# A two-layer decoder trunk on one core: fill steps laid otherwise, y gated and stored in the next head, values' weights split earlier, late weights loaded into another tile

## The chip, the cores and the metric

The kernel runs on one core of a Trainium2 chip. The time is device time in microseconds, the median of several runs; a profiled execution has a time and a trace of its own.

## The reference, cut to what matters

Two pre-norm residual layers on x of 1024 positions by 1024 channels, then a final RMSNorm. Layer 0 is a recurrent layer (RG-LRU); the change does not touch it. Layer 1 is forgetting attention with 16 heads of 64:

```python
u = h @ w_in                          # h = rms_norm(x): queries, keys, values, gate, forget logits
cum = jnp.cumsum(log_sigmoid(f_logit + b_f), axis=1)
logits = q @ k.T / 8 + (cum_q - cum_k), causal mask
p = softmax(logits)                   # per head, 1024 x 1024
o = p @ v
y = o * silu(gate)
x = x + y @ w_out
```

All is float32. The kernel takes every large product in three passes on TensorE: each operand is split into a high part (a cast, `to_hi`) and a low part (a subtraction, `to_lo`).

## The kernel before, in words

**Heads and runs.** Layer 1 loops over 16 heads (line 1116). Queries fall into two chunks of 512, c=0 and c=1, a chunk into four score rows of 128 queries. Head hd has two runs. The first weighs chunk 0 of the head (`weigh(hd, 0)`) beside the score rows 7, 6, 5, 4 of its chunk 1 (`maxima(hd, 1)`); the second weighs chunk 1 beside the score rows 3, 2, 1, 0 of the next head's chunk 0.

**The order on TensorE is written out by hand.** `ordered` walks a string: `1` is the next step of `maxima` (one score row), `0` the next step of `weigh`, `.` the next step of a generator of other work, `fill`; every matmul of a step is queued behind the last one before (`tc.issue_after(pe[0].ins)`). A fill step is six matmuls of 128x512. In heads 0 to 11 the fill is the next pair's keys, queries and gate (`kq_units`, `g_units`), 12 steps a head; later it is the output projection's partial products (`partial`). After a dot the generator `side` also takes a step.

**`maxima`, a score row:** four or two matmuls into a PSUM tile S; VectorE masks and takes the maximum in one instruction (L773); ScalarE takes the exponential with the row's sum (L778). Rows 6, 7 and 2, 3 are also turned: a block transpose on VectorE (L733), a store to DRAM, and four loads back (`pp<-turnd`, L745). The PSUM tag S has two buffers, which score rows and transposes share in turn.

**`weigh`:** its steps come in two kinds. Near rows are transposed by TensorE into a PSUM tile (`pt`), split by a cast `ph` and a subtraction `pl` (both listed as lines 87 and 98, the helpers `to_hi` and `to_lo`), and multiplied by the values in the step after. Far rows come from the DMA, are split in one step and multiplied in the next; their casts are queued behind the last exponential (`seen`), their subtractions behind the last maximum (`masked`). At the end the output is copied and added into `yo` (L903, L904).

**Gating.** `fetch_sums` loads the reciprocal sums, broadcast to 64 partitions; `scale` multiplies the gate by them and `gated` the output by the gate, both on GpSimd (L813, L913). `put_away` casts and subtracts an odd head's y and stores both parts in DRAM. Before, `settle` (beside the second run) fetches at its third step and scales and gates chunk 0 at its fourth; chunk 1 is gated after the run; the stores come in the next head's first run, at the dots 3 and 5.

**Values.** Before heads 4, 8 and 12, `values` computes the values of the next four heads. `value_weights` loads their weights in four quarters and splits each a step later.

**Weights' buffers.** All weights are loaded into the tag `wf` of three buffers and split into `wh` and `wl`, four buffers in `wpool`, two in `vwpool`. In head 14's second run `late` loads and splits, in four steps, the part of the output weights that the last pair needs.

**Queues.** Every DMA is issued by SP, in one queue, in order. The framework lists each engine's instructions ahead of time by a simulated time; it may place a load earlier than the code's order when its buffer is free.

Of the kernel before, what the change touches and what calls it, by code (L numbers as in the profile page):

```python
# [11 lines left out]
F32 = mybir.dt.float32  # L12
# [5 lines left out]
P = 128  # L18
SEQ = 1024
HALF = 512  # L20
# [3 lines left out]
HD = 64  # L24
EPS = 1e-6
GROUP = 2
ORDER = "1.0.1.10.1..0", "10.1.0.10.1.0.0"
LAST = "1..0.1..10..1..0", "10..1.0..10..1.0..0"
NEG = -1e30
PSUM = bass.MemoryType.PSUM  # L30
# [3 lines left out]
def f32(ap):  # L34
    return ap.bitcast(F32)
# [3 lines left out]
def trunk(ctx: ExitStack, tc: tile.TileContext, xt, w0, wg, wo0, pc, gn, gf, w1, wv, wf, bf, wo1, out):  # L39
    nc = tc.nc  # L40

    def pool(name, bufs, **kw):
        return tc.tile_pool(name=name, bufs=bufs, **kw)
# [7 lines left out]
    wpool = ctx.enter_context(pool("w", 4))  # L51
# [32 lines left out]
    def to_hi(hi, src, eng, scale=None):  # L84
        if eng is nc.scalar:
            if scale is None:
                nc.scalar.copy(hi, src)  # L87
            else:
                nc.scalar.activation(hi, src, AF.Copy, scale=scale)
        elif eng is nc.gpsimd:  # L90
            nc.gpsimd.tensor_scalar(hi, src, 1.0 if scale is None else scale, 0.0, ALU.mult, ALU.add)
        elif scale is None:
            eng.tensor_copy(hi, src)
        else:
            eng.tensor_scalar(hi, src, scale, None, ALU.mult)

    def to_lo(lo, src, hi, eng):
        return eng.tensor_tensor(lo, src, f32(hi), ALU.subtract)  # L98
# [80 lines left out]
    with ExitStack() as l0:  # L179
# [35 lines left out]
        k = 0  # L215
# [11 lines left out]
        def split_x(h, layer=0):  # L227
            for k, (hi, lo) in enumerate((raw, hT)[layer][h]):
                g_ = gnt[:, layer, k : k + 1]
                x = xs[h][k]  # L230
                to_hi(hi, x, nc.scalar, scale=g_)
                nc.vector.scalar_tensor_tensor(lo, x, g_, f32(hi), ALU.mult, ALU.subtract)  # L232
                yield
# [217 lines left out]
        vwpool = late.enter_context(pool("vw", 2, side="right"))  # L451
# [17 lines left out]
        for h, cs in enumerate(halves):  # L469
            y = [tuple(z[:, cs] for z in p) for p in ys[-2:]]  # L470
            hT[h] = [pair() for k in range(KT)]
            parts = split_x(h, 1)
# [29 lines left out]
    with ExitStack() as l1:  # L502
        tu = l1.enter_context(pool("tu", 1))
        at = l1.enter_context(pool("at", 2))
# [22 lines left out]
        def value_weights(g, parts):  # L527

            waiting = []
            for k in range(0, KT + 2, 2):  # L530
                if k < KT:
                    wt = wpool.tile([P, 2, 256], F32, tag="wf", name="wf", bufs=3)
                    nc.sync.dma_start(wt, wv[g, :, k : k + 2])
                    waiting.append(wt)
                if k:
                    own = wpool if k <= 4 else vwpool
                    hi = own.tile([P, 2, 256], F32R, tag="wh", name="wh")
                    lo = own.tile([P, 2, 256], F32R, tag="wl", name="wl")
                    with tc.issue_after(seen[0].ins):
                        to_hi(hi, waiting[0], nc.scalar)  # L540
                    with tc.issue_after(masked[0].ins):
                        to_lo(lo, waiting.pop(0), hi, nc.vector)
                    parts += [(hi[:, i], lo[:, i]) for i in range(2)]
                yield

        def values(g, parts):

# [260 lines left out]
        def scale(hd, cs=slice(0, SEQ)):  # L808
            rows = slice((hd % 2) * HD, (hd % 2 + 1) * HD)
            for b in range(cs.start, cs.stop, HALF):  # L810
                part = slice(b, b + HALF)
                sg = sgs[hd // 2][rows, part]
                nc.gpsimd.tensor_tensor(sg, sg, recs[hd // 2][rows, part], ALU.mult)  # L813
# [93 lines left out]
        def gated(hd, c, sub=slice(0, HALF)):  # L907

            if hd % 2 == 0:
                return  # L910
            pair = hd // 2
            yo = yos[pair, c][:, sub]
            nc.gpsimd.tensor_tensor(  # L913
                yo, yo, sgs[pair][:, c * HALF + sub.start : c * HALF + sub.stop], ALU.mult
            )
            if hd == 15:
                split_y(c, pair, yo, sub)

        def put_away(hd, c):
            if hd % 2 == 0 or hd > 12:  # L920
                return
            pair = hd // 2
            yo = yos[pair, c]
            yh = at.tile([P, HALF], F32R, tag="xp", name="yh", bufs=2)
            with tc.issue_after(seen[0].ins):
                to_hi(yh, yo, nc.scalar)
            with tc.issue_after(masked[0].ins):
                to_lo(yo.bitcast(F32R), yo, yh, nc.vector)
            for part, y in enumerate((f32(yh), yo)):
                nc.sync.dma_start(y1d[c, pair, part], y)  # L930

        def settle(hd):
            yield
            yield
            with tc.issue_after(written[0].ins):
                fetch_sums(hd)
            yield
            scale(hd)
            gated(hd, 0)

        def put_later(hd):
            for c in range(2):
                yield
                yield
                put_away(hd, c)

        def beside(*gens):
            for _ in itertools.zip_longest(*gens):
                yield
# [5 lines left out]
        def chain(*gens):  # L955
            for g in gens:
                yield from g
# [21 lines left out]
        def split_y(c, pair, y, sub=slice(0, HALF)):  # L979
            yh, yl = (z[:, sub] for z in (pair_of_y(c, pair) if sub.start == 0 else y1[c][pair]))  # L980
            to_hi(yh, y, nc.scalar)
            to_lo(yl, y, yh, nc.vector)
# [102 lines left out]
        def late():  # L1085

            for half in range(2):
                wh, wl = (kqpool.tile([P, 8, P], F32R, tag=f"qk{p}{half}", name=f"wo{p}") for p in "hl")
                for b in range(2):
                    wt = wpool.tile([P, 4, P], F32, tag="wf", name="wf", bufs=3)  # L1090
                    for d in range(2):
                        nc.sync.dma_start(wt[:, 2 * d : 2 * d + 2], wo1[half * 4 + b * 2 + d, :, 6:8])
                    sl = slice(4 * b, 4 * b + 4)

                    with tc.issue_after(seen[0].ins):
                        to_hi(wh[:, sl], wt, nc.scalar)
                    to_lo(wl[:, sl], wt, wh[:, sl], nc.vector)
                    yield
                late_w.append((wh, wl))
# [16 lines left out]
        for hd in range(HEADS):  # L1116
            pair = hd // 2
            if hd % 2 == 0:
                if hd < 12:
                    fill = kq_units(pair + 1, ((1, (0, 1)), (0, (0,))))  # L1120
                elif hd == 12:
                    pairs = ((0, 1), (2, 3), (4, 5), (6, 7))
                    todo = [(db, c) for two in pairs for c in range(2) for db in two]
                    fill = chain(
                        kq_units(7),
                        g_units(7, (0,)),
                        load_y(0),
                        first_out(),
                        g_units(7, (1,)),
                        load_y(1),  # L1130
                        partial(todo),
                        turned(0, 0),
                        turned(0, 1),
                    )
            elif pair < 6:
                fill = chain(kq_units(pair + 1, ((0, (1,)),)), late_q(hd + 1), g_units(pair + 1))
            first, second = LAST if hd > 11 else ORDER
            side = put_later(hd - 1) if hd else iter(())
            run(first, weigh(hd, 0), maxima(hd, 1), fill=fill, side=side)
            drain(side)  # L1140
            if hd == HEADS - 1:
                break
            if hd == 14:
                with tc.issue_after(seen[0].ins):
                    split_y(1, 6, yos[6, 1])
                scale(hd)
            side = late() if hd == 14 else settle(hd)
            if hd % 4 == 3 and hd < 12:

                parts = []  # L1150
                side = beside(side, value_weights(hd // 4 + 1, parts))
            run(second, weigh(hd, 1), maxima(hd + 1, 0), fill=fill, side=side)
            drain(side)
            gated(hd, 1)
            if hd == 13:
                with tc.issue_after(seen[0].ins):
                    split_y(0, 6, yos[6, 0])
            if hd < 12:
                drain(fill)
            if hd % 4 == 3 and hd < 12:  # L1160
                drain(values(hd // 4 + 1, parts))
            if hd + 2 < HEADS:
                load(hd + 2, us=(0,) if hd % 2 == 0 and hd < 12 else (0, 1))
# [84 lines left out]
```

## Time and profile before

| | |
|---|---|
| median of 3 runs | 1116.9 us (1115.07 to 1117.86) |
| the profiled execution: its time, its span | 1114.79 us, 1113.0 us |
| TensorE granted clock, mean | 0.995 |
| TensorE, VectorE, ScalarE, GpSimd busy | 98%, 71%, 52%, 15% of the span |
| DMA traffic | 145.81 MB, mean 131 GB/s |

The span runs from the first instruction to the last. A matmul's end is modelled and reaches into the next one's start, so that a busy TensorE may still lose a few tenths of a microsecond here and there; stalls are best read from start to start. In the lists of waits a line names who waited, on which line of the code, for whom, then the total, the number of times and the longest, in us. In the timeline a line has the start, the duration, the engine, the code's line, the instruction, what it writes and reads, its shape, how many were merged, and in brackets the idle time before it and what ended it. Two rows are merged where they follow each other on their engine.

### The profile page before, as it was taken

Reading aid. Unit: us, or ns where it says so; the run is one execution under the profiler, and the core shown is the slowest. Engines: PE = TensorE matmul, PEld = TensorE weight load, DVE = VectorE, ACT = ScalarE, POOL = GpSimd, SP = SyncE. Lnnn points to the kernel's source line nnn. Section 1 sums busy time; section 2 is a strip of 40 time slices with the busy share of each in tenths; the row PEclk is TensorE's granted clock in tenths of the full one; section 3 lists DMA queues with packets and bytes.
Section 4 is the critical chain, followed back from the end, with each engine's and each line's share of the span. In section 5 each row is a group of like instructions: output and inputs, shape, how many; then the busy total and the mean of one; then the engine's idle time right before and its main releaser. Section 6 shows DMA issues by size and latency. Waiting matters only on the chain.

```text
span 1113.0 us, 15892 instructions
## 1 busy us (share of the span) xinstructions
PE 1088.5 (98%) x5645; PEld 921.1 (83%) x5645; DVE 792.1 (71%) x1280; ACT 579.9 (52%) x1037; POOL 171.8 (15%) x120
## 2 busy tenths in 40 slices
PE   9999999999999999999999999999999999998997
PEld 7787888888888888987888888788888898887886
DVE  8888755876569787757887478874788757666445
ACT  8487345355454665545555355553556535434335
POOL 2312212111121201420121101111012110110010
PEclk9999999999999999999999999999999999999999
DMA  6111111111112113445767357674477845785344
GB/s 220 62 53 42 52 53 48 48 54 45 43 48 71 48 65 116 130 124 162 199 192 195 118 161 193 200 198 123 150 189 213 198 126 166 248 266 174 109 147 189
DMA packets 100919, 145.81 MB, mean 131 GB/s; under 512 B 25348, under 2 KB 53636, under 8 KB 100840
## 3 DMA queue, kind: packets, MB, share of 16 engines
q1 hardware_dynamic: 100840, 144.80, 43.6%
q8 instruction: 44, 0.72, 0.3%
q14 instruction: 35, 0.29, 0.1%
HBM read 83.48 MB, written 36.11 MB: 107 GB/s over the span
## 4 chain that ended last, share of the span: by engine, by line
PE 76%; DVE 7%; DMA 6%; issue 5%; ACT 4%; SPq 1%; POOL 1%; ACTq 0%; DVEq 0%; POOLq 0%
PE gps L57 26%; PE ops L57 16%; PE ups L57 10%; PE vps L57 7%; PE S L57 5%; PE O L57 4%; PE gate L57 3%; PE turn L57 2%; PE pt L61 2%; DVE pl L98 2%; ACT pp L778 1%; DMA T<-qkl 1%; DVE S L773 1%; DMA U<-qkh 1%; DMA turnd<-turn 1%
## 5 line engine op out<-in xcount | busy, mean ns | idle before, releaser
L57 PE MATMUL gps<-hh,wh 128*128 128x512 f32 x576 | 229.4, 398 | 0.0
L57 PE MATMUL gps<-hh,wl 128*128 128x512 f32 x576 | 225.6, 392 | 0.2 <-POOL wl L98 0.2
L57 PE MATMUL gps<-hl,wh 128*128 128x512 f32 x576 | 225.1, 391 | 0.0
L87 ACT CAST wh<-wf 128x512 fp32r<-128x512 f32 (+2 forms) x156 | 94.2, 607 | 138.0 <-PE ops L57 43.1
L98 POOL TENSOR_TENSOR wl<-wf,wh 128x512 fp32r<-128x512 f32 (+1 forms) x60 | 99.5, 1664 | 378.1 <-ACT wh L87 260.3
L57 PEld LDWEIGHTS gps<-hl,wh 128*128 128x128 f32 x576 | 108.2, 188 | 23.6
L57 PEld LDWEIGHTS gps<-hh,wl 128*128 128x128 f32 x576 | 108.7, 189 | 18.7 <-POOL wl L98 0.6
L57 PEld LDWEIGHTS gps<-hh,wh 128*128 128x128 f32 x576 | 108.5, 188 | 18.5
L813 POOL TENSOR_TENSOR sg<-sg,recb 64x512 f32<-64x512 f32 x32 | 44.4, 1407 | 487.6 <-DMA recb<-recd 445.7
L773 DVE CUSTOM_DVE_ANT_0 S<-S,mask 128x512 f32<-128x512 f32 (+7 forms) x128 | 97.0, 758 | 24.7 <-PE S L57 24.4
L778 ACT ACTIVATE pp<-S,m 128x512 f32<-128x512 f32 (+1 forms) x64 | 54.4, 851 | 87.9 <-DVE m L773 87.8
L57 PE MATMUL S<-T,U 128*128 128x512 f32 (+7 forms) x384 | 92.6, 350 | 4.0 <-ACT pp L778 4.0
L98 DVE TENSOR_TENSOR wl<-wf,wh 128x512 fp32r<-128x512 f32 x96 | 68.6, 720 | 22.6 <-ACT wh L87 22.5
L57 PEld LDWEIGHTS S<-T,U 128*128 128x128 f32 (+1 forms) x384 | 67.5, 190 | 20.8 <-ACT pp L778 9.1
L375 DVE TENSOR_TENSOR x<-x,ops 128x512 f32<-128x512 f32 x80 | 54.1, 680 | 41.2 <-PE ops L57 41.2
L57 PE MATMUL O<-pl,v 128*128 128x256 f32 (+3 forms) x302 | 77.2, 290 | 2.2 <-DMA T<-qkl 1.2
L57 PE MATMUL O<-ph,v 128*128 128x256 f32 (+3 forms) x302 | 78.8, 289 | 0.0
L57 PE MATMUL ups<-hh,wl 128*128 128x512 f32 x192 | 75.3, 392 | 0.8 <-POOL wl L98 0.8
L57 PE MATMUL ups<-hh,wh 128*128 128x512 f32 x192 | 75.7, 395 | 0.0
L57 PE MATMUL ups<-hl,wh 128*128 128x512 f32 x192 | 75.2, 392 | 0.2 <-DVE hl L232 0.2
L57 PE MATMUL vps<-wh,hh 128*128 128x256 f32 (+1 forms) x256 | 73.3, 287 | 2.0 <-DVE v L575 1.0
L57 PE MATMUL ops<-yh,wh 128*128 128x512 f32 x192 | 75.2, 392 | 0.0
(170 smaller groups left out, 2372.3 us busy)
## 6 DMA issues: line engine op xcount, KB each, us to landing
wf<-in_w SPq DMA_DIRECT2D x100, 256.0 KB
turnd<-turn SPq DMA_DIRECT2D x26, 448.0 KB
pp<-turnd SPq DMA_DIRECT2D x52, 224.0 KB
wf<-in_wo SPq DMA_DIRECT2D x64, 128.0 KB
U<-qkh SPq DMA_DIRECT2D x64, 128.0 KB
T<-qkh SPq DMA_DIRECT2D x28, 256.0 KB
turnd<-turn SPq DMA_DIRECT2D x13, 384.0 KB
pp<-turnd SPq DMA_DIRECT2D x52, 96.0 KB
```

The source lines that it names most:

```text
L57: pe[0] = nc.tensor.matmul(*args, **kw)
L61: pe[0] = nc.tensor.transpose(*args)
L87: nc.scalar.copy(hi, src)
L98: return eng.tensor_tensor(lo, src, f32(hi), ALU.subtract)
L375: nc.vector.tensor_tensor(x, x, pt, ALU.add)
L773: masked[0] = nc.vector.tensor_tensor_reduce(S[:, :n], S[:, :n], mask[:, SEQ - n :], -1.0, -NEG, ALU.add, ALU.min, accum_out=m)
L778: seen[0] = nc.scalar.activation(p, S[:, :n], AF.Exp, bias=m, scale=-1.0, accum_out=sums[:, i : i + 1])
L813: nc.gpsimd.tensor_tensor(sg, sg, recs[hd // 2][rows, part], ALU.mult)
```

## The change

- `ORDER`, the strings of heads 0 to 11, has the same steps with dots at other places: in the first run one dot moves from between the fourth score row and the last step of `weigh` to between the first step of `weigh` and the second score row; in the second run one moves from before the fourth step of `weigh` to between its first step and the second score row.
- For heads up to 11, `scale` and `gated` move from the end of the head to the first dot of the next one; the stores of y go to its fourth dot and the end of its first run.
- `value_weights` takes seven steps instead of five, the first five of them beside the head's first run. The first two quarters are split into `vwpool` and the last two into `wpool`, the other way round than before.
- In `late`, the first and third load go into the tile `turn`, which before held the score rows on their way to DRAM and is not used after head 12's second run.

```diff
-ORDER = "1.0.1.10.1..0", "10.1.0.10.1.0.0"
+ORDER = "1.0..1.10.1.0", "10..1.0.10.10.0"
...
                 if k:
-                    own = wpool if k <= 4 else vwpool
+                    own = vwpool if k <= 4 else wpool
...
                 yield
+                if k < 4:
+                    yield
...
-        def put_away(hd, c):
-            if hd % 2 == 0 or hd > 12:
+        def store_y(hd, c):
+            if hd % 2 == 0:
                 return
...
             with tc.issue_after(written[0].ins):
                 fetch_sums(hd)
-            yield
+            if hd > 11:
+                yield
+                scale(hd)
+                gated(hd, 0)
+
+        def put_away(hd):
             scale(hd)
-            gated(hd, 0)
-
-        def put_later(hd):
             for c in range(2):
-                yield
-                yield
-                put_away(hd, c)
+                gated(hd, c)
+            for c in range(2):
+                yield
+                yield
+                yield
+                store_y(hd, c)
...
                 for b in range(2):
-                    wt = wpool.tile([P, 4, P], F32, tag="wf", name="wf", bufs=3)
+                    if b:
+                        wt = wpool.tile([P, 4, P], F32, tag="wf", name="wf", bufs=3)
+                    else:
+                        wt = at.tile([P, 7 * P], F32, tag="turn", name="wf", bufs=1)[:, :HALF]
+                        wt = wt.rearrange("p (d j) -> p d j", j=P)
...
-            side = put_later(hd - 1) if hd else iter(())
+            side = put_away(hd - 1) if 0 < hd < 13 else iter(())
+            if hd % 4 == 3 and hd < 12:
+                parts = []
+                coming = value_weights(hd // 4 + 1, parts)
+                side = beside(side, itertools.islice(coming, 5))
             run(first, weigh(hd, 0), maxima(hd, 1), fill=fill, side=side)
...
             if hd % 4 == 3 and hd < 12:
-
-                parts = []
-                side = beside(side, value_weights(hd // 4 + 1, parts))
+                side = beside(side, coming)
             run(second, weigh(hd, 1), maxima(hd + 1, 0), fill=fill, side=side)
             drain(side)
-            gated(hd, 1)
+            if hd > 11:
+                gated(hd, 1)
```

## The prediction

> **What bounds the kernel now.** I read the page first, then the waits of all engines and of TensorE alone, then the timeline around each long TensorE wait.
>
> ```profile
> PE 1088.5 (98%) x5645; PEld 921.1 (83%) x5645; DVE 792.1 (71%) x1280; ACT 579.9 (52%) x1037; POOL 171.8 (15%) x120
> ```
>
> TensorE is busy 98% of the span of 1113.0 us, and the change adds and removes no matmul. All that can be won are the times in which TensorE waits. They are few:
>
> ```profile
> POOL sg L813 <- DMA recb<-recd: 445.7, 16, 45.5
> ACT wh L87 <- DMA wf<-in_w: 14.4, 7, 4.3
> PE S L57 <- ACT pp L778: 4.0, 8, 1.1
> PE ops L57 <- ACT wh L87: 3.2, 1, 3.2
> PE vps L57 <- DVE wl L98: 2.2, 3, 0.9
> PE vps L57 <- ACT wh L87: 0.6, 1, 0.6
> PE O L57 <- DMA T<-qkl: 1.2, 2, 0.7
> PE O L57 <- DVE pl L98: 0.7, 1, 0.7
> ```
>
> The columns are total us, times, longest. The reader is to see six small groups, and that none belongs to the first layer, which the change leaves alone. I count a stall from start to start, less the usual distance of two matmuls: that gives some 0.2 us more per wait than these rows, since a matmul's modelled end runs into the wait.
>
> I name the steps of a head so: S7 to S0 are the score rows (7 to 4 in the first run, 3 to 0 in the second), T a transpose step, P a product step of `weigh`, a dot one fill step. A fill step is six matmuls (a row of the chain of waits; 1.39 from start to start):
>
> ```profile
> 579.09 1.40 PE gps L57 x6
> ```
>
> **The change, part by part.**
>
> **A. Late weights.** Two of the four loads of `late()` leave the `wf` ring of three buffers for the `turn` tile, which nothing uses after head 12's second run. The timeline there:
>
> ```profile
> 1021.21 1.27 DVE L98 TENSOR_TENSOR wol<-wf,woh 128x512 fp32r<-128x512 f32 x2
> ...
> 1022.87 1.05 SPq L1092 DMA_DIRECT2D wf<-in_wo  x2
> 1024.01 1.29 SPq L108 DMA_DIRECT2D wf<-in_wo  x2
> ...
> 1025.18 0.39 PE L57 MATMUL ops<-yhl,wh 128*128 128x512 f32 x1
> 1028.72 0.79 PE L57 MATMUL ops<-yhh,wh 128*128 128x512 f32 x1 [3.15 <-ACT wh L87]
> 1029.98 0.79 PE L57 MATMUL ops<-yhh,wl 128*128 128x512 f32 x1 [0.47 <-DVE wl L98]
> ...
> 1027.47 0.62 ACT L87 CAST woh<-wf 128x512 fp32r<-128x512 f32 x1 [2.26 <-DMA wf<-in_wo]
> 1028.05 0.93 ACT L87 CAST wh<-wf 128x512 fp32r<-128x512 f32 x2
> ```
>
> The output weights of block 5 (L108) are loaded only at 1024.01, because the fourth late load (L1092, 1022.87) and they queue for ring buffers that the casts at 1021.21 give back. ScalarE then waits 2.26 us for that late load with block 5's cast behind it. TensorE loses 3.54 - 0.23 = 3.3 us, then 1.26 - 0.23 = 1.0 us. Then it runs slowly:
>
> ```profile
> 1028.70:1034.60 5.90, 5.41 (x16) 4.36 (x17) 2.05 (x5) 0.95 (x4) 0.08 (x1) 0.50 0.50 172
> ```
>
> The granted clock (third number from the end) is 0.50; of the 5.9 us 1.3 is the wait just counted, and the other 4.6 us would have taken 2.3 at full clock: 2.3 us lost. Together 6.6 us.
>
> After the change the ring serves late 2, late 4 and block 5: two of these find a buffer as soon as block 4's weights are split, long before 1021, so that the fourth late load no longer stands in front. What is late next is late 3: `turn` has one buffer, so its load waits for the first late subtraction (1021.87, the first of the pair at 1021.21), comes some 3 us later, and ScalarE may wait for it with block 5's cast behind. Bounds: 6.6 gone, or only the 1.1 us by which block 5's load moves up to 1022.9 (with a like share of the rest, 1.5). Loads here are placed ahead of the code's order when their buffer is free, so I take a value near the first: **-5.5 us**. The two loads cost no more issue time on SP than before.
>
> **B. The values' weights.** Before heads 4, 8 and 12, four quarters are loaded, cast and subtracted beside the second run, the last at its fifth dot. At the end of that run:
>
> ```profile
> 618.43 0.62 ACT L87 CAST wh<-wf 128x512 fp32r<-128x512 f32 x1 [3.39 <-DMA wf<-in_w]
> ...
> 619.31 0.61 ACT L87 CAST wh<-wf 128x512 fp32r<-128x512 f32 x1
> ...
> 620.49 0.38 PE L57 MATMUL O<-ph,v 128*128 128x256 f32 x1
> 621.79 0.39 PE L57 MATMUL vps<-wl,hh 128*128 128x256 f32 x1 [0.91 <-DVE wl L98]
> ```
>
> The last quarter's cast (619.31) stands behind a cast that waits 3.39 us for the next head's weights; the loss is 1.30 - 0.12 = 1.2 us. The wait row above has it three times with 2.2 us; with the same 0.3 added to each, and the one wait of `vps` for `wh`, 3.9 us in all. Now two quarters are split in the first run and two at the second run's first two dots, so the values' weights are there some five dots (7 us) ahead. I let a quarter of the 3.9 stand, for the cast that waits for the next head's weights is still there and holds back S0's exponential: **-2.9 us**. The price: two casts (0.62 each on ACT) and two subtractions (0.64 each on DVE, half of the pair at 1021.21) per such head into the first run, beside S6 to S4; and on SP three of the four loads come ahead of the gate's weights, whose second half then takes its ring buffer only after the first quarter is split. I hold that hidden: it is needed only at the seventh dot, after the whole first run. Bounds: -3.9, and +3.9 if it is not hidden (a rival below). Buffers: the first two quarters take the pool whose last use lies a group of heads back, the last two the free half of the other; no new wait.
>
> **C. Fill steps laid otherwise.** The first run moves a dot from before the last P to between T and S6; the second one from before P2 to between T and S2. What the even heads have there now (the first row is an odd head's, for comparison):
>
> ```profile
> 683.64 1.02 DVE L98 TENSOR_TENSOR pl<-pp,ph 128x512 fp32r<-128x512 f32 x2
> ...
> 704.79 0.40 PE L57 MATMUL gps<-hl,wh 128*128 128x512 f32 x1
> 706.26 1.09 PE L57 MATMUL S<-T,U 128*128 128x512 f32 x4 [1.07 <-ACT pp L778]
> ...
> 718.15 0.27 PE L791 MATMUL tr<-ident,sums 128*8 128x128 f32 x1
> 718.82 0.62 PE L57 MATMUL S<-T,U 128*128 128x384 f32 x2 [0.39 <-ACT pp L778]
> ...
> 715.77 0.58 ACT L903 COPY yo<-O 64x512 f32<-64x512 f32 x1 [0.39 <-DMA y1d<-yo]
> 717.97 0.70 ACT L778 ACTIVATE pp<-S,m 128x512 f32<-128x512 f32 x1
> ...
> 728.36 2.12 DVE L98 TENSOR_TENSOR pl<-pp,ph 128x512 fp32r<-128x512 f32 x2 [1.33 <-ACT ph L87]
> 728.80 2.83 POOL L813 TENSOR_TENSOR sg<-sg,recb 64x512 f32<-64x512 f32 x2 [23.57 <-DMA recb<-recd]
> ```
>
> S6 and S2 wait for the exponential of the row that holds their PSUM buffer (1.24 and 0.6 us). Of such waits the list has 8 with 4.0 us, with 0.2 added to each 5.6. A dot more (1.39) covers every one: **-5.6 us**. At the end of the head the pair of subtractions takes 2.12 us beside GpSimd's two, against 1.02 without (683.64), and the last P waits: the two last rows of the list, three heads, 2.5 us with the addition. P2 and with it these subtractions now come up to a dot earlier against GpSimd, which starts when the sums' DMA lands; I take **-1.6 us** of the 2.5.
>
> What is late next: the products that lose their dot. An odd head, which has none of these waits (the last two rows are an even head's):
>
> ```profile
> 679.51 0.86 PE L57 MATMUL S<-T,U 128*128 128x512 f32 x4
> 685.42 0.28 PE L57 MATMUL O<-ph,v 128*128 128x256 f32 x1
> ...
> 693.89 0.40 PE L57 MATMUL S<-T,U 128*128 128x256 f32 x2
> 697.60 0.28 PE L57 MATMUL O<-ph,v 128*128 128x256 f32 x1
> ...
> 695.95 0.69 DVE L98 TENSOR_TENSOR pl<-pp,ph 128x512 fp32r<-128x512 f32 x1 [1.14 <-ACT ph L87]
> ...
> 708.57 0.86 PE L57 MATMUL S<-T,U 128*128 128x512 f32 x4
> 713.30 1.02 DVE L98 TENSOR_TENSOR pl<-pp,ph 128x512 fp32r<-128x512 f32 x2
> ```
>
> First run: from S5 (679.51) to the last P (685.42) are 5.91 us, after the change 4.52. Its second matmul needs the first low part, ready at S5 + 4.82 (half of the pair at 683.64), so it waits 4.82 + 0.07 - 4.64 = 0.25 us. In even heads the store of y puts a subtraction before it, and it is ready at S5 + 5.4 (708.57 and half of the pair at 713.30): up to 0.85. Second run: from S1 (693.89) to P2 (697.60) 3.71, after it 2.32; the low part is ready at S1 + 2.75 (695.95 + 0.69), so the second matmul waits 2.82 - 2.44 = 0.4, and a later one 0.1: 0.5. For heads 1 to 11 first runs: six odd at 0.25, five even at 0.55, 4.25 us. Second runs: nine heads at 0.5, 4.5 us; in the other three, matmuls of the values stand between. **+8.75 us.** Bounds: nothing (the low part ahead of the next row's maximum, as would be possible on VectorE), or the whole dot at twenty places, 27.8. I take the rows' own distances. Sum of C: -5.6 - 1.6 + 8.75 = **+1.5 us**.
>
> **D. Gating and stores of y.** Moved in the code, `scale` and `gated` are not moved in time: the wait row of POOL shows that it stands idle until the sums land, with nothing else in its queue, and the fetch keeps its place at the third dot behind the same store on SP. **0.** The stores do move, c=0 by one dot, c=1 to the end of the run: two casts, two subtractions, four DMAs per pair, none new. The copy at 715.77 already waits 0.39 us for the first store; it waits up to 1.4 longer, and behind it on ScalarE stand the casts of T and S3's exponential (717.97). S2 waits for that, but now has its extra dot: covered, just. Without that cover it costs 0.5 in five heads.
>
> Sum: -5.5 - 2.9 + 1.5 = -6.9 us on this execution, whose own time was 1114.79: 1107.9. The median of the three runs, 1116.9, is 2.1 above it, so the forecast is **1110.0 us**.
>
> **The rivals.**
>
> 1. *The products become the bound; slower.* At the twenty places of C the low parts come later than now, because the moved fill brings its own subtraction and cast in front of them. For it: VectorE is busy 71% overall and has no gap between S5's maximum and the pair at 683.64. Against it: the moved work is the same amount. A and B and the removed waits give 15.6 us; slower by 0.3% (3.35 us) needs 19 us of new waits, 0.95 at each place. At the full dot, 27.8, it ends at 1116.9 + 12.2 = 1129.
> 2. *`turn` is the new queue.* Late 3 stands in front of block 5 on ScalarE; the stall falls only from 3.3 to about 2, the rest in proportion: A is -2.7 and the time 1112.8. The single buffer speaks for it, the early placing of loads against it. [...]
> 3. *The early values' loads hold the ring.* The gate's second half comes late in heads 3, 7 and 11; the row of ScalarE's waits for `wf<-in_w` (7 times, up to 4.3) shows such casts. With 1.3 us each, 4.3 less a margin of 3, B is +3.9 at most and the time 1116.8: no change.
> 4. *No new waits.* VectorE's order falls well and C is -7.2: 1101.3.
>
> **How the numbers follow.** Forecast 0.55 (1105 to 1113.5), rival 1 0.08, rival 2 0.14, rival 3 0.13, rival 4 0.10. A measurement of this kernel can tell about 0.3%, 3.35 us. Faster by more: the forecast, rival 4 and most of rival 2, 0.76. Within: rival 3 and the rest, 0.16. Slower: 0.08. The range 1102.5 to 1116 leaves out rival 1 and the end of rival 4.
>
> **What would show it.** A: no wait of `ops` for `wh` near 1025 and a clock of 1.00 there. B: no `vps` wait for `wl`. C: no `S` wait for `pp` in S6 and S2, and new waits of `O` for `pl`, about 0.25 to 0.5 each in every head; if these are absent, or near 1.4, C is wrong. D: POOL's scaling still starts beside the head's last subtractions (728.80 now). The prediction fails if the late stall stays or the `O` waits exceed 0.9.

## The result, and the profile after

The changed kernel takes **1112.0 us** (median of 5 runs, 1110.89 to 1113.33), the kernel before, run beside it, 1116.9 (1115.07 to 1118.11). The ratio is 0.9961, 95% interval 0.9947 to 0.9975: faster by 4.4 us (2.8 to 5.9). The forecast was 1110.0 in a range of 1102.5 to 1116. The profiled execution after had a time of 1113.33 and a span of 1111.6 us; that of before, 1114.79, lay below all of those five runs, so the two traces differ by 1.5 us only.

TensorE's waits after, over the whole span (columns as before: total us, times, longest):

```profile
PE O L57 <- DVE pl L98: 10.5, 24, 0.7
PE turn L57 <- DVE xp L1016: 1.7, 1, 1.7
PE O L57 <- ACT ph L87: 1.3, 2, 0.8
```

No row is left of `S` waiting for `pp`, of `vps` for `wl` or `wh`, of `ops` for `wh`. In their place stands the first row, products that wait for their low parts, in nearly every head. The late weights first, from the timeline and from the table by stretches (its third number from the end is the granted clock):

```profile
1021.76 0.62 ACT L87 CAST wh<-wf 128x512 fp32r<-128x512 f32 x1 [0.34 <-DMA wf<-in_wo]
...
1031.72 0.62 ACT L87 CAST woh<-wf 128x512 fp32r<-128x512 f32 x1 [2.09 <-DMA wf<-in_wo]
```

```profile
1028.00:1034.00 6.00, 6.00 (x32) 5.13 (x31) 4.11 (x6) 3.21 (x8) 2.53 (x2) 1.00 0.83 255
```

Block 5's weights are cast at 1021.76 (1028.05 before), TensorE is busy in all of the 6 us, at full clock. The last late load still comes 2.09 us late, but nothing that TensorE needs soon stands behind it. A first run after (head 5), VectorE's and TensorE's rows:

```profile
682.01 0.86 PE L57 MATMUL S<-T,U 128*128 128x512 f32 x4
...
684.83 0.65 DVE L98 TENSOR_TENSOR wl<-wf,wh 128x512 fp32r<-128x512 f32 x1
685.39 0.68 DVE L614 SCALAR_TENSOR_TENSOR qkl<-gps,qkh 128x512 fp32r<-128x512 f32 x1
686.00 0.82 DVE L775 CUSTOM_DVE_ANT_0 S<-S,mask 128x640 f32<-128x640 f32 x1
686.74 1.02 DVE L98 TENSOR_TENSOR pl<-pp,ph 128x512 fp32r<-128x512 f32 x2
...
687.48 0.39 PE L57 MATMUL O<-pl,v 128*128 128x256 f32 x1 [0.65 <-DVE pl L98]
```

The first low part is ready 5.4 us after S5 began (686.74 and the 0.69 of one such subtraction, less 682.01; the product that waits for it starts at 687.48), not 4.82 as in the same head before: the fill step that moved brings its weights' subtraction (`wl`) and its result's (`qkl`) in front of the row's maximum on VectorE. And the end of head 3:

```profile
614.61 0.40 PE L57 MATMUL S<-T,U 128*128 128x256 f32 x2
...
615.96 0.62 ACT L87 CAST wh<-wf 128x512 fp32r<-128x512 f32 x1 [4.20 <-DMA wf<-in_w]
...
616.61 0.69 DVE L98 TENSOR_TENSOR wl<-wf,wh 128x512 fp32r<-128x512 f32 x1 [3.93 <-ACT wh L87]
...
617.22 0.42 DVE L775 CUSTOM_DVE_ANT_0 S<-S,mask 128x256 f32<-128x256 f32 x1
...
617.74 0.48 ACT L780 ACTIVATE p<-S,m 128x256 f32<-128x256 f32 x1 [1.16 <-DVE m L775]
...
618.87 0.39 PE L57 MATMUL O<-ph,v 128*128 128x256 f32 x1 [0.81 <-ACT ph L87]
...
619.59 0.38 PE L57 MATMUL O<-pl,v 128*128 128x256 f32 x1 [0.34 <-DVE pl L98]
...
621.28 0.58 PE L57 MATMUL O<-pl,v 128*128 128x256 f32 x1 [0.73 <-DVE pl L98]
```

The values' weights are there in time, but the cast of the next head's weights waits 4.20 us (3.39 before). VectorE stands idle 3.93 us for the subtraction that follows this cast, with S1's maximum queued behind it: S1's matmuls begin at 614.61, the maximum only at 617.22, the exponential at 617.74. TensorE then waits three times before products, for their high or low parts.

The account of the two traces: within the heads (480 to 935 us) the wait rows of before sum to 10.9 us in 19 waits, those after to 12.3 in 27. With the 0.2 us a wait of the prediction's count that is +3.0; 1.4 more for a half clock at 621 to 624 (below), 0.8 for the longer `turn` wait, and -6.6 for the late weights: -1.4, as the spans say.

### The profile page after: what moved, and what is told of

The parts are those of the page before. It is cut to its first block, busy times and chain, and to the rows that moved or that the text cites. A ratio compares the mean times of both kernels' runs of the same rounds, so it can differ in the third digit from the quotient of the medians.

```text
span 1111.6 us, 15903 instructions
## 1 busy us (share of the span) xinstructions
PE 1088.2 (98%) x5645; PEld 921.9 (83%) x5645; DVE 785.4 (71%) x1280; ACT 581.3 (52%) x1037; POOL 175.2 (16%) x120
## 4 chain that ended last, share of the span: by engine, by line
PE 75%; DMA 8%; DVE 7%; issue 5%; ACT 3%; SPq 1%; POOL 1%; ACTq 0%; DVEq 0%; POOLq 0%
PE gps L57 24%; PE ops L57 16%; PE ups L57 10%; PE vps L57 8%; PE O L57 5%; PE S L57 4%; PE gate L57 3%; PE turn L57 2%; DMA pp<-turnd 2%; PE pt L61 2%; DMA wf<-in_w 2%; DVE pl L98 2%; DMA turnd<-turn 1%; DVE turn L735 1%; DVE S L775 1%
## 5 line engine op out<-in xcount | busy, mean ns | idle before, releaser
L98 POOL TENSOR_TENSOR wl<-wf,wh 128x512 fp32r<-128x512 f32 (+1 forms) x60 | 101.9, 1705 | 376.0 <-ACT wh L87 261.4
L57 PE MATMUL O<-pl,v 128*128 128x256 f32 (+3 forms) x302 | 80.3, 301 | 10.8 <-DVE pl L98 10.5
L98 DVE TENSOR_TENSOR wl<-wf,wh 128x512 fp32r<-128x512 f32 x96 | 64.9, 677 | 30.7 <-ACT wh L87 30.5
L57 PE MATMUL ops<-yh,wl 128*128 128x512 f32 x192 | 74.7, 389 | 0.0
```

Of the source, the lines that this page charges most:

```text
L57: pe[0] = nc.tensor.matmul(*args, **kw)
```

## The experiments

All times are against runs of the kernel before on the same chip; times per part in us are the ratio's distance from 1 on 1116.5.

### Each of the four parts alone

The late weights' second buffer (A):

```
+  if b: wt = wpool.tile(..., tag="wf", bufs=3)
+  else: wt = at.tile([P, 7 * P], F32, tag="turn", name="wf", bufs=1)[:, :HALF]
```

> The kernel before, with only two of the four late loads moved to the tile turn. Theory (each part keeps its own sum): the stall at the fifth block of output weights and the half clock behind it go, -6 us with a price of up to 0.8 us at the final transposes; ratio 0.9945 to 0.996. Rival (the late part needs the other layout to pay): within 2 us of before, ratio above 0.998.

Measured: 1109.53 us, ratio 0.9944 (0.9931 to 0.9957): -6.3 us, and the `ops` wait is gone.

The order strings (C):

```
-ORDER = "1.0.1.10.1..0", "10.1.0.10.1.0.0"
+ORDER = "1.0..1.10.1.0", "10..1.0.10.10.0"
```

> The kernel before, with only the two strings of the fill steps changed. Theory: the new waits of products for their low parts (0.8 us in the first run of eight heads, 0.4 to 0.8 in the second run of twelve) outweigh the waits of score rows that go (some 6 us) and of the last products (some 2.5): slower by 3 to 6 us, ratio 1.003 to 1.005. Rival (the layout pays, and the missing gain is in the values): faster by 1 to 3 us, ratio 0.997 to 0.999.

Measured: 1115.56 us, ratio 1.0007 (0.9992 to 1.0023). Its largest row of waits, over the heads:

```profile
PE O L57 <- DVE pl L98: 10.7, 20, 1.5
```

One set of waits is exchanged for another of about the same size (all rows: 11.4 us in 23, against 10.9 in 19 before); neither side's number was met. The waits of `vps` for `wl` and `wh` are gone here too, without B. Four of its twelve executions, the profiled one among them, took over 1120 us at a mean clock of 0.989 to 0.991, the others 1112.4 to 1116.6 at 0.992 to 0.997. In the profiled one the granted clock falls behind the waits at the ends of heads 3, 7 and 11 (0.53 from 624 to 627 us, 0.52 and 0.51 from 764 to 771, 0.58 from 907 to 910), where the trace before has 1.00 in every stretch from 480 to 1015.

The values' weights half a head sooner (B):

```
-                    own = wpool if k <= 4 else vwpool
+                    own = vwpool if k <= 4 else wpool
...
+                if k < 4:
+                    yield
...
+                coming = value_weights(hd // 4 + 1, parts)
+                side = beside(side, itertools.islice(coming, 5))
             run(first, ...)
```

> The kernel before, with only the values' weights split half a head sooner. Theory: the wait of the values for their own low parts goes, but ScalarE still stands at the next head's weights in front of the second run's last exponentials, so that products wait instead: 0 to -2 us, ratio 0.998 to 1.0. Rival (the forecast): -2.9 us, ratio 0.9974.

Measured: 1125.61 us, ratio 1.0083 (1.0064 to 1.0101): **9.3 us slower**, a miss. TensorE's waits in the heads, then ScalarE's row of waits for weights in the same stretch, and the timeline at the end of head 2:

```profile
PE S L57 <- ACT pp L780: 8.1, 13, 1.8
PE O L57 <- DVE pl L98: 7.7, 13, 1.0
```

```profile
ACT wh L87 <- DMA wf<-in_w: 29.5, 8, 5.4
```

```profile
557.07 0.36 SPq L533 DMA_DIRECT2D wf<-in_wv  x1
...
563.01 0.36 SPq L533 DMA_DIRECT2D wf<-in_wv  x1
563.47 0.39 SPq L108 DMA_DIRECT2D wf<-in_w  x1
...
578.09 0.70 SPq L108 DMA_DIRECT2D wf<-in_w  x1
...
582.91 0.62 ACT L87 CAST wh<-wf 128x512 fp32r<-128x512 f32 x1 [3.87 <-DMA wf<-in_w]
583.44 0.57 ACT L780 ACTIVATE pp<-S,m 128x384 f32<-128x384 f32 x1
...
584.15 0.50 PE L57 MATMUL S<-T,U 128*128 128x256 f32 x2 [0.28 <-ACT pp L780]
...
585.37 0.38 PE L57 MATMUL O<-pl,v 128*128 128x256 f32 x1 [0.36 <-DVE pl L98]
```

Two values' loads (L533) go out ahead of the weights that are needed first, and hold two of the three `wf` buffers. Before, weights went out at 556.42 and 562.40 and a values' load only behind them:

```profile
556.42 0.36 SPq L108 DMA_DIRECT2D wf<-in_w  x1
...
562.40 0.36 SPq L108 DMA_DIRECT2D wf<-in_w  x1
562.86 0.40 SPq L533 DMA_DIRECT2D wf<-in_wv  x1
```

With B the second one goes at 578.09, and the cast for it holds S2's exponential (583.44), and with it S1 and its product, back on ScalarE. All wait rows of the heads sum to 18.1 us in 29 waits, against 10.9 in 19 before: with 0.2 a wait 9.2 us more. Behind the waits at the end of head 7 the clock is at 0.50 (769.2 to 772), some 1.7 us more; together they are about the 10.6 us by which this trace's span, 1123.6, exceeds that of before.

Gating and stores of y in the next head (D):

```
-        def put_later(hd):
+        def put_away(hd):
+            scale(hd)
             for c in range(2):
+                gated(hd, c)
+            for c in range(2):
                 yield
                 yield
-                put_away(hd, c)
+                yield
+                store_y(hd, c)
```

> The kernel before, with only scaling, gating and the stores of y moved to the next head in the code. Theory: GpSimd runs when the sums land, whatever the place in the code: no change, within 1.5 us, and GpSimd's scaling as long after the fetch as before. Rival: the later store makes the next pair's first copy wait on ScalarE, and score row 2 waits for the exponential behind it: slower by 2 us or more, ratio above 1.0018.

Measured: 1125.34 us, ratio 1.0081 (1.0068 to 1.0094): **9.0 us slower**, a miss for the theory; the rival, 2 us or more, holds. ScalarE's row for stores in the heads, then the same place in the timeline:

```profile
ACT yo L903 <- DMA y1d<-yo: 14.1, 5, 3.2
```

```profile
574.48 2.58 SPq L745 DMA_DIRECT2D pp<-turnd  x4
577.10 0.60 SPq L930 DMA_DIRECT2D y1d<-yo  x1
...
581.97 0.58 ACT L903 COPY yo<-O 64x512 f32<-64x512 f32 x1 [3.21 <-DMA y1d<-yo]
...
583.10 0.58 ACT L778 ACTIVATE pp<-S,m 128x384 f32<-128x384 f32 x1
...
583.82 0.50 PE L57 MATMUL S<-T,U 128*128 128x256 f32 x2 [0.23 <-ACT pp L778]
...
585.58 0.39 PE L57 MATMUL O<-pl,v 128*128 128x256 f32 x1 [0.90 <-DVE pl L98]
```

The third step ahead of a store puts the store of `yo` on SyncE behind the four read-backs `pp<-turnd`, which take 2.58 us to issue. The copy into that buffer waits 3.21 us, and a cast and S2's exponential queue behind it; S1 and its product wait in turn. ScalarE took them one after the other in this trace: the copy at 581.97, the cast at 582.45, the exponential at 583.10.

### Is that what B and D cost?

D with two steps instead of three:

```
                 yield
                 yield
-                yield
                 store_y(hd, c)
```

> The kernel before with the changed gating and stores of y alone, but with two steps instead of three ahead of each store (the store-only kernel, slower by 9 us, had three). Theory: its 9 us came from the third step. In its trace the first y1d<-yo of head 2 goes out at 577.10, behind the four pp<-turnd of SyncE's queue, where the kernel before sent it at 572.07, ahead of them; ScalarE's copy yo<-O into the same buffer then waits 3.21 us at 581.97 (five such waits, 14.1 us in all; before two, 0.7 us), and everything queued behind it on ScalarE is late. With two steps the stores stand on SyncE's queue as they did before: ratio 0.998 to 1.002, no yo wait for y1d above 1 us. Rival: the cost is of gating both halves at the head of the next head (the POOL scaling beside VectorE), and stays: ratio 1.006 to 1.009.

Measured: 1117.33 us, ratio 0.9999 (0.9988 to 1.0011). SyncE's rows show the store ahead of the read-backs, as it was before the change, and no wait of `yo` for `y1d` is left:

```profile
571.32 0.32 SPq L930 DMA_DIRECT2D y1d<-yo  x1
...
573.06 2.58 SPq L745 DMA_DIRECT2D pp<-turnd  x4
```

So the 9 us were the third step; moving the gating costs nothing that these runs can tell.

B begun two steps later:

```
-                side = beside(side, itertools.islice(coming, 5))
+                side = beside(side, itertools.chain([None] * 2, itertools.islice(coming, 3)))
```

> The kernel before with the values' split alone, begun two steps later in the first run (the values-only kernel, slower by 9 us, began it at once). Theory: its 9 us are rival 3 of the prediction. In its trace the values' loads go out at 557.07 and 563.01 and hold two of the three wf buffers, the query weights' load follows at 578.09 and ScalarE's cast wh<-wf waits for it 3.87 us at 582.91 (six such waits in heads 0 to 11, 27.3 us; before three, 11.0 us). Held two steps, both weights' loads of the fill stand ahead of the second values' load: the waits near 583, 725 and 870 go, and with them the S waits of up to 1.94 us in the second runs there; ratio 0.996 to 1.001. Rival: the cost lies in the exchanged split buffers or in VectorE's order, and stays: ratio 1.006 to 1.009.

Measured: 1116.88 us, ratio 0.9999 (0.9987 to 1.0012). ScalarE's row for weights in the heads falls from 29.5 us to:

```profile
ACT wh L87 <- DMA wf<-in_w: 8.2, 4, 3.7
```

So the 9.3 us were the early loads, not the exchanged buffers; and without them B gains nothing either. At the ends of heads 3, 7 and 11 the waits of the values for their weights mostly became waits of products: 4.0 us in six waits, against 3.7 in seven before.

### The parts together

A and C:

> The late weights' second buffer and the new layout of the fill steps together, without the other two parts. If the parts add as they measured alone (0.9944 and 1.0007): ratio 0.995, some 1110.5 us, and the changed kernel's other two parts together cost about 1 us there. Rival: the new layout gains once the other parts are in, and alone spoils the gain of the late weights: ratio 0.997 or more.

Measured: 1109.15 us, ratio 0.9929 (0.9917 to 0.9940).

A, C and D (the changed kernel without B):

> The changed kernel without its earlier split of the values' weights: late weights, new layout, gating and stores of y in the next head. Theory: in the new layout the stores with three steps stand ahead of the read-backs on SyncE (y1d<-yo at 572.22 in the changed kernel's trace, against 577.10 in the store-only kernel), so that part costs nothing there: the same as late weights and layout alone within 0.2%, ratio 0.994 to 0.996. Rival: it costs its 9 us in any layout and the values' split pays for it in the changed kernel: ratio 1.001 to 1.004.

Measured: 1111.03 us, ratio 0.9942 (0.9928 to 0.9956). Where C is in, D costs 0.13%, too little for these intervals to tell from nothing. B on top of it, the changed kernel, has 0.9961: 2 us more, with intervals that overlap a little.

The changed kernel with the old layout (A, B and D):

> The changed kernel with the old layout of the fill steps. Theory: the waits of ScalarE that the values' split and the three-step stores brought alone (for wf near 583, 725, 870; for y1d near 582, 666, 724, 810, 870) come back, and the layout is what hid most of them: slower than before, ratio 1.011 if they add (0.9944, 1.0083, 1.0081), some 1.003 where they fall into the same stretch of ScalarE's queue and only the longer one counts. Rival: the two parts cost nothing once they are together, in any layout: 0.994 to 0.996.

Measured: 1116.48 us, ratio 0.9997 (0.9981 to 1.0013). The rival is out, and the theory's numbers, 1.011 and 1.003, were not met either. ScalarE's row for stores in the heads, and the place in head 2 again:

```profile
ACT yo L905 <- DMA y1d<-yo: 14.2, 5, 3.2
```

```profile
581.15 0.58 ACT L905 COPY yo<-O 64x512 f32<-64x512 f32 x1 [2.66 <-DMA y1d<-yo]
...
582.97 0.62 ACT L87 CAST wh<-wf 128x512 fp32r<-128x512 f32 x1
```

D's wait is back in full. B's is not: its cast now stands behind the waiting copy, and by 582.97 its load has come. Past A's gain, B and D cost 5.9 us here together (0.9997 against 0.9944), less than either alone. So single ratios can't be multiplied: the product of the four is 1.0115, the changed kernel 0.9961, and **C is worth nothing alone (1.0007) and 4 us in the company of the others** (0.9961 against 0.9997). In the changed kernel the first store of `yo` is ahead of the read-backs again, since the new first run has its fourth dot, at which the store stands, a score row sooner; and the cast waits, but 1.60 us and not 3.87 as with B alone, and no score row waits for S2's exponential behind it:

```profile
572.22 0.32 SPq L932 DMA_DIRECT2D y1d<-yo  x1
...
573.98 2.58 SPq L747 DMA_DIRECT2D pp<-turnd  x4
...
582.22 0.62 ACT L87 CAST wh<-wf 128x512 fp32r<-128x512 f32 x1 [1.60 <-DMA wf<-in_w]
```

### A version that beats both

In the old layout the even heads wait and the odd ones don't, but for the values at the ends of heads 3, 7 and 11; in the new one nearly every head does. So: A, with the new layout in even heads and the old one in odd heads.

```
+ORDER = ("1.0..1.10.1.0", "10..1.0.10.10.0"), ("1.0.1.10.1..0", "10.1.0.10.1.0.0")
...
+            first, second = LAST if hd > 11 else ORDER[hd % 2]
```

> Late weights' second buffer, and the fill layout chosen by the head's parity: the changed layout in even heads, the old one in odd heads. From the traces of late weights alone and of late weights with the new layout: with the old layout the waits of some 0.6 + 0.6 + 0.8 us fall in the even heads (566.92, 579.49, 591.79) and none in the odd ones; with the new layout some 0.8 + 0.38 us in every head except 3, 7 and 11. If a head's waits go with its own layout, even heads cost 1.2 us and odd heads nothing: some 3 to 4 us below either, ratio 0.990 to 0.992. Rival: a head's waits come from the layout of the head before it (its fill is queued there), and move into the odd heads: ratio 0.993 to 0.996.

Measured: **1104.55 us, ratio 0.9895** (0.9880 to 0.9909), a little below what the theory gave. TensorE's waits in the heads, all of its rows:

```profile
PE vps L57 <- DVE wl L98: 2.0, 2, 1.4
PE O L57 <- DVE pl L98: 1.9, 7, 0.6
PE vps L57 <- ACT wh L87: 1.6, 2, 0.8
PE vps L57 <- DVE v L575: 0.6, 2, 0.3
PE pt L61 <- ACT pp L778: 0.5, 1, 0.5
```

6.6 us in 14 waits, against 10.9 in 19 before: a head's waits go with its own layout. It came out below the theory because the even heads wait less than they do with the new layout throughout: of the waits in their first runs one is left (0.60 in head 2).

The same with the old first run in all heads, the new second run in even ones:

> Late weights' second buffer, the old layout in every first run, and the changed layout only in the second run of even heads. If the S wait of 0.60 us in the second run of even heads (579.49) and the O wait behind it (0.8 us in head 2, 0.22 in others) turn into one O wait of 0.38 us: about 0.5 us a pair, 3 us below late weights alone, ratio 0.991 to 0.993. Rival: the second run hands its late casts to the next first run, nothing gained: ratio 0.994 to 0.996.

Measured: 1106.40 us, ratio 0.9912 (0.9895 to 0.9928), as expected. And the layout by parity with B held two steps:

> As the layout by parity, with the values' weights split from the third step of the first run on. If holding the loads two steps leaves the query weights' loads ahead, the ends of heads 3, 7 and 11 lose the 0.7 to 1.0 us that TensorE waits there for casts of the values' weights: up to 2 us below the layout by parity, ratio 0.988 to 0.991. Rival, as with the held split alone (0.9999): waits for casts of the values' weights turn into waits of O for pl at the same place, no gain: the same as the layout by parity within 0.1%.

Measured: 1104.12 us, ratio 0.9896 (0.9882 to 0.9911). The rival holds: B gains nothing here either.

## Why the prediction was right, and where it was wrong

**A (-5.5): right.** -6.3 us alone (-4.8 to -7.7), so rather its upper bound of 6.6. (Its lower bound of 1.5 leaves out the half clock; a like share of that too makes it 2.2. The measurement is far from both.) `turn`'s single buffer did make the last late load late, as said, but block 5's cast stands ahead of it; rival 2 did not happen. The clock stayed at 1.00 (1015 to 1045, with A alone and in the changed kernel).

**The sum of the other parts (-1.4): too good, and by the middle values wrong in sign.** The change less A alone is +1.9 us (0.9961 against 0.9944; the two intervals overlap a little). That is 3.3 us worse than forecast, A was 0.8 better, and the 2.5 left are what lies between the forecast of -6.9 and the measured -4.4. So the time fell into the range through A; and that B and D, which cost 9 us each alone, didn't push it out was luck: past A they cost 5.9 us together in the old layout, and C's layout, chosen for other waits, takes 4 of these away.

**B (-2.9): the step that failed** is "I let a quarter of the 3.9 stand". All `vps` waits for `wl` and `wh` did go (they go with C alone too, so this sign doesn't tell B), but with the cast for the next head's weights at 4.20 us the last maximum and exponentials took their place as what is late last: products wait 0.81, 0.34 and 0.73 us in head 3, and at the ends of heads 3, 7 and 11 together 4.4 us in nine waits, against 3.7 in seven before. The prediction names that cast and prices it at a quarter; the whole stood. Held two steps, B is worth 0.0 alone and 0.0 in the best version. The second failed step is "I hold that hidden" for the loads: rival 3 saw the ring but looked in heads 3, 7 and 11 at the gate's weights. Loads are placed ahead of the code when a buffer is free, which the prediction uses for A and forgot here; with B alone the first two values' loads go out at 557.07 and 563.01, about a head ahead of head 3, where the code has them, and displace a weight load of head 2. Alone that costs 9.3 us against a bound of 3.9.

**C (+1.5): mechanism right, sizes off both ways.** The `S` waits went, the new `O` waits came, none above 0.73. In first runs the low part is late in odd heads as well, 5.4 us after S5 where 4.82 was taken from before (683.64 and one subtraction's 0.69, not "half of the pair"). So eight heads, odd and even, wait 0.65 us, 6.8 in all with 0.2 added to each, for the 4.25 of the sum; the second runs' nine waits, 0.21 or 0.36, are 4.1 so counted, for 4.5. The dot that moves brings its own two subtractions, which is what rival 1 says, at a smaller price. Alone C measured +0.8 (-0.9 to +2.6).

**D (0): right in the changed kernel, for a reason given only as a cover.** "Without that cover it costs 0.5 in five heads" was mis-sized: the store does not move by one dot but past the four read-backs on SyncE, the wait is 3.2 us and not 1.4 longer than 0.39, and alone D costs 9.0 us. The prediction did list the queue, and did not ask what stands between the two places.

Not settled: that B costs 2 us in the changed kernel rests on two intervals that overlap. The waits at the ends of heads 3, 7 and 11 don't show it: 4.4 us in nine with B, 5.3 in five without, about the same with 0.2 added to each; only the half clock behind head 3 is in the trace with B and not in the other. And the trace of D alone is 10.7 us longer than that of before. Its waits in the heads, 16.5 us in 26, give 7 by the count above, and the half clock behind the waits of head 7 (0.56, 0.50, 0.50 and 0.73 in the four us from 769) 1.7; where the other 2 fall was not found.

## What to carry to other kernels

When a load or store is moved by a step, list what stands between its old and new place on its queue and which ring buffer it takes, then ask who overwrites or waits for that buffer: two moves that look free cost 9 us each here, both in ScalarE's queue, where S2's exponential ran only behind a late cast (582.91, then 583.44) or a late copy (581.97, then 583.10). Parts of a change that meet in one queue did not add here (a product of 1.0115, a measured 0.9961); run them alone and in company before you keep or drop one. And look per head, not per kernel: two layouts that differed by less than 2 us on the whole gave some 4 to 5.5 us more when each was used in the heads in which it does not wait.

## What the runs showed of the hardware that was not expected

TensorE's clock fell to half without a long wait. The end of head 3 in the changed kernel, by stretches:

```profile
617.60:619.30 1.70, 0.84 (x5) 0.44 (x4) 0.56 (x3) 1.56 (x4) 0.35 (x1) 1.00 0.49 175
619.30:621.00 1.70, 0.96 (x6) 0.75 (x6) 1.70 (x4) 1.19 (x6) 1.70 (x2) 0.93 0.48 125
621.00:624.00 3.00, 2.72 (x8) 2.33 (x9) 3.00 (x4) 0.73 (x3) 2.92 (x2) 0.50 0.77 196
```

No wait is longer than 0.81 us, but TensorE was busy in only 1.80 of 3.40 us, and then ran 3 us at 0.50: 1.4 us lost (half of 2.72). The prediction counts a half clock only behind the wait of 3.15 us at the late weights; here the same followed three short waits close together.

Nor does a low busy share bring the half clock every time. With A and C together, at the end of head 7:

```profile
761.60:765.01 3.41, 1.12 (x5) 0.72 (x5) 3.41 (x4) 0.60 (x2) 2.45 (x2) 1.00 0.80 218
```

TensorE was busy in only 1.12 of 3.41 us there, and the clock stayed at 1.00, as it is from 740 to 780 as a whole. What decides between such stretches stays open here.
